# Moving the second block's context norm, keys and values from a layer's MLP to its attention

## The chip, the cores and the metric

One core of a Trainium2 chip runs the whole program as one launch. The metric is device microseconds of one execution, taken as the median over runs; lower is better. The engines of the core are TensorE (PE in the profile, its weight loads shown apart as PEld), VectorE (DVE), ScalarE (ACT), GpSimd (POOL) and SyncE (SP), whose queue issues nearly all DMA transfers. Each engine works through its own instructions in the order in which the program lists them for it.

## The reference, cut to what matters

Two transformer blocks run one after the other on 512 tokens of width 1024. The first has two layers: in each, three kinds of attention (sliding window, full grouped-query, and latent attention called MLA) over 512 latent and 256 context tokens, and a squared-ReLU MLP. The second block starts with differential attention beside a long convolution. Its attention also sees 256 context tokens of its own, `ctx_2`. What the change touches is only this: the norm of that context, and the keys and values made from it.

```python
a_ctx = _modulate(_rmsnorm(h_ctx, norm1_g[i]), mod_c[0], mod_c[1])          # 256 x 1024
kv_ctx = a_ctx @ mix_w_in[e][:, KV_START:HY_START] + mix_b_in[e][KV_START:HY_START]
k_c, v_c = _split_kv(kv_ctx)                                                # 256 x 512 each
k_all = jnp.concatenate([k_c, k_l], axis=1)
v_all = jnp.concatenate([v_c, v_l], axis=1)
```

`ctx_2` and the modulation depend on nothing that the first block computes, so this work may stand anywhere before the second block's attention.

## The kernel before, in words

Activations lie transposed, with 128 channels on the partitions and tokens along the free side; a 1024-wide vector is eight such tiles. Large products are made from a high and a low part of each operand (`mm3`, L645: hi·hi, hi·lo, lo·hi). Their weights are streamed in tiles of 128x1024: SP issues the load of `wraw` (L72), ACT casts the high part `whi` (L90), DVE subtracts for the low part `wlo` (L91). The context keys and values are the exception: they are plain fp32 matmuls with unsplit weights. One such matmul instruction on 256 columns shows as two records in the trace.

The program is written as generators that are stepped in turn, and a scheduler then fixes each engine's instruction list by the order of writing and priorities. Tiles come from pools with fixed numbers of slots, and a tile whose slot is still in use by an earlier one waits for the last user of that one: the large pool `B` has 21 slots, `Tm` (scratch of one 128x512 tile) four, `wm` (tiles of modulation weights) two. In PSUM, during the first block's attention, there are two double banks and four single ones (`P1`).

**Attention of the second layer** (about 1200 to 1400 us) is a list of 64 units, each a head and a stretch of queries. `attend` walks it with a lag: scores `s` (L257, mask L259) on PE, maximum and sums `st` on DVE, exponential `p` (L280) on ACT, normalisation `p` (L289) on POOL, transposes `pt` (L303) on PE, a high and a low copy `pth` (L330, ACT) and `ptl` (L335, DVE), the product `acc` with the values (L346), and its evacuation through a `Tm` tile `yt` (L349, ACT), an ACT copy `y` (L351) and a POOL addition (L352). Between units it calls `fill(i)`, which steps preparations: `prepare(p)` forms queries and keys of the MLA heads (`cn`, `cx`, `ck`, scratch tiles `w` and `u` in `Tm`, DMAs into `qc` and `kc`). Units 0 to 15 are full attention, 16 to 31 the window, 32 to 63 MLA.

**The MLP of that layer** (about 1505 to 1845 us) is stepped by `run(mlp, 0.8, 1.3)`: per step of the MLP it makes 0.8 steps of the modulation jobs and 1.3 steps of `self.jobs`, which `queue2` has filled with the filter of the long convolution and then `context_job`. That job loads `ctx_2` into two `B` tiles, sums squares (`RmsNorm.feed`: `rq` L203, `ns` L211, then sums over the channels on PE, `rv` L208 and L209), forms the inverse root (L632 to L637), applies norm and modulation (L1492 DVE, L1493 POOL), and makes the keys of four heads: eight matmuls each (L1502), bias into `ckx` (L1505, ACT), high and low parts stacked in `ckk` (L1553 ACT, L1554 DVE), a DMA to DRAM (`kctx`). Weights come by `SideStream` (tiles `wside`, each load paced by a small POOL copy).

**The transition** from that MLP to the second block (about 1863 to 1901 us) is a layer norm followed by the second block's own RMS norm. The loop over `self.side` steps it, and in between steps `context_values`: 32 matmul instructions (L1532, two double PSUM tiles), bias `cvx` (L1537, DVE), split `cvv` (L651 ACT, L652 DVE), DMA to `vctx`. Then the second block's projections `pj` begin.

## Time and profile before

| | before |
|---|---|
| median of three runs | 2979.42 us (2972.44 to 2990.2) |
| profiled execution | 2984.58 us, its span 2982.6 us |
| mean granted TensorE clock | 0.979 |
| PE busy | 2822.2 us, 95% of the span |
| DVE busy | 1973.3 us, 66% |
| ACT busy | 1235.4 us, 41% |
| POOL busy | 640.3 us, 21% |

The rows further down are read against the profiled execution. Busy time counts an engine's instructions, not its waits; a granted clock of 1.00 is TensorE's upper level (2.4 GHz), 0.50 its lower one (1.2 GHz). In a view of the chain, each step of the program's critical path is one line with its start and length; a step on PE that follows another on PE without a gap means that PE itself was the limit there.

### The profile page before, as it was taken

To read this page: it belongs to the slowest core of one execution; us is meant where nothing else is said; L and a number is where in the kernel's file an instruction comes from. 1 tells how busy PE (TensorE), PEld (TensorE's weight loads), DVE (VectorE), ACT (ScalarE), POOL (GpSimd) and SP (SyncE) were. 2 spreads that over 40 slices of the span, in tenths; PEclk is the share of its full clock that TensorE was granted. 3 is DMA by queue.
4 is the path that set the end of the run, shared out by engine and by line. 5 is a ranking of instruction groups with operands and counts; after the bars stand their busy time and mean duration, and the time that the engine had idled before them with its cause. 6 is when DMAs were issued, how large, how long until landed. Compare 5 with 4: busy or idle time off the path is not lost.

```text
span 2982.6 us, 40376 instructions
## 1 busy us (share of the span) xinstructions
PE 2822.2 (95%) x15212; PEld 2373.5 (80%) x15212; DVE 1973.3 (66%) x3193; ACT 1235.4 (41%) x2249; POOL 640.3 (21%) x780
## 2 busy tenths in 40 slices
PE   8988999999999989898999999998899999999998
PEld 5877778888888877777887788777688888888887
DVE  3677777775657476887687565768976754664445
ACT  3477663322222244776332332533653223543322
POOL 1034346300000061343601121312310000200001
PEclk8999999999999999999999999999999999999999
DMA  6022222344434221012145455233115542222222
GB/s 252 32 68 71 90 89 85 107 145 157 143 113 142 78 71 47 13 37 70 64 170 182 166 205 187 97 125 117 64 64 193 202 139 99 76 78 94 97 99 71
DMA packets 102218, 327.95 MB, mean 110 GB/s; under 512 B 11617, under 2 KB 18721, under 8 KB 102024
## 3 DMA queue, kind: packets, MB, share of 16 engines
q1 hardware_dynamic: 101448, 323.67, 31.3%
q8 instruction: 120, 1.97, 0.3%
q10 hardware_dynamic: 576, 1.71, 0.2%
q14 instruction: 74, 0.61, 0.1%
HBM read 306.98 MB, written 12.59 MB: 107 GB/s over the span
## 4 chain that ended last, share of the span: by engine, by line
PE 75%; DVE 11%; ACT 5%; issue 4%; DMA 2%; POOL 2%; DVEq 0%; ACTq 0%; POOLq 0%; SPq 0%
PE f L645 48%; PE pj L645 7%; PE op L645 5%; PE s L257 3%; PE acc L346 2%; PE pt L303 1%; DVE ptl L335 1%; DVE st L270 1%; DVE h L1088 1%; ACT p L280 1%; DVE wlo L91 1%; ACT pth L330 1%; PE ms L1112 1%; PE lv L180 1%; DVE R L174 1%
## 5 line engine op out<-in xcount | busy, mean ns | idle before, releaser
L90 ACT CAST whi<-wraw 128x1024 fp32r<-128x1024 f32 x342 | 357.6, 1046 | 1211.0 <-PE f L645 1000.7
L645 PE MATMUL f<-hn,whi 128*128 128x512 f32 (+1 forms) x2688 | 718.1, 365 | 8.3 <-ACT hn L1089 6.8
L91 DVE TENSOR_TENSOR wlo<-wraw,whi 128x1024 fp32r<-128x1024 f32 x342 | 422.8, 1237 | 325.7 <-ACT whi L90 319.1
L645 PE MATMUL f<-act,whi 128*128 128x512 f32 x2240 | 612.2, 371 | 1.6 <-DVE R L990 1.6
L645 PEld LDWEIGHTS f<-hn,whi 128*128 128x128 f32 x2688 | 467.0, 190 | 93.0 <-ACT hn L1089 8.0
L645 PEld LDWEIGHTS f<-act,whi 128*128 128x128 f32 x2240 | 388.9, 188 | 77.1 <-DVE R L990 2.8
L645 PE MATMUL f<-hn,wlo 128*128 128x512 f32 (+1 forms) x1344 | 447.3, 362 | 0.0
L645 PE MATMUL f<-act,wlo 128*128 128x512 f32 x1120 | 377.6, 370 | 0.0
L990 DVE SCALAR_TENSOR_TENSOR R<-f,modsb,R 128x512 f32<-128x512 f32 (+1 forms) x280 | 188.9, 693 | 161.2 <-PE f L645 160.9
L645 PEld LDWEIGHTS f<-hn,wlo 128*128 128x128 f32 x1344 | 239.2, 190 | 40.2
L574 DVE SCALAR_TENSOR_TENSOR wm<-wm,sbc 128x1024 f32<-128x1024 f32 x152 | 188.9, 1246 | 119.6 <-DMA wm<-wada_in 75.5
L645 PE MATMUL pj<-h,whi 128*128 128x512 f32 (+1 forms) x912 | 248.0, 372 | 11.1 <-ACT h L651 5.4
L564 POOL COPY wm<-act 128x1 f32<-128x1 f32 x144 | 78.7, 554 | 792.0 <-DVE wm L574 388.1
L645 PEld LDWEIGHTS f<-act,wlo 128*128 128x128 f32 x1120 | 195.4, 188 | 37.1
L645 PEld LDWEIGHTS pj<-h,whi 128*128 128x128 f32 x912 | 158.5, 193 | 47.3 <-issue 7.4
L289 POOL TENSOR_SCALAR p<-p,st 128x768 f32<-128x768 f32 (+2 forms) x160 | 130.3, 817 | 226.8 <-DVE st L287 180.8
L270 DVE TENSOR_REDUCE st<-s 128x1 f32<-128x768 f32 (+3 forms) x176 | 156.3, 889 | 31.2 <-PE s L257 19.3
L335 DVE TENSOR_TENSOR ptl<-pt,pth 128x256 fp32r<-128x256 f32 (+3 forms) x304 | 153.3, 535 | 18.8 <-ACT pth L330 15.4
L211 POOL TENSOR_TENSOR ns<-ns,rq 128x256 f32<-128x256 f32 x54 | 46.3, 867 | 479.8 <-ACT rq L203 478.7
L303 PE MATMUL pt<-ident,p 128*128 128x128 f32 x816 | 124.6, 281 | 23.1 <-DVE ptl L335 9.7
L645 PE MATMUL pj<-h,wlo 128*128 128x512 f32 (+1 forms) x456 | 145.5, 359 | 0.0
L280 ACT ACTIVATE p<-s,st 128x768 f32<-128x768 f32 (+2 forms) x160 | 125.8, 788 | 44.6 <-DVE st L270 34.3
(377 smaller groups left out, 4629.4 us busy)
## 6 DMA issues: line engine op xcount, KB each, us to landing
wraw<-fc_in SPq DMA_DIRECT2D x128, 512.0 KB, 3.4
wraw<-mlp_in SPq DMA_DIRECT2D x128, 512.0 KB, 3.2
wm<-wada_in SPq DMA_DIRECT2D x96, 512.0 KB, 4.0
wm<-wmod_in SPq DMA_DIRECT2D x56, 512.0 KB, 4.0
wraw<-win_in SPq DMA_DIRECT2D x24, 512.0 KB, 3.2
wm<-wmodk_in SPq DMA_DIRECT2D x24, 512.0 KB, 4.4
wn<-wmodk_in SPq DMA_DIRECT2D x16, 512.0 KB, 8.6
wraw<-wout_in SPq DMA_DIRECT2D x16, 512.0 KB, 3.2
```

What stands on the lines that cost most here:

```text
L90: nc.scalar.copy(out=hi[:, 0:n], in_=t[:, 0:n])
L91: nc.vector.tensor_tensor(out=lo[:, 0:n], in0=t[:, 0:n], in1=hi[:, 0:n].bitcast(F32), op=ALU.subtract)
L257: nc.tensor.matmul(self.s[:, a:b], lhsT=q, rhs=kk[:, k0:k0 + b - a], start=i == 0, stop=end)
L270: nc.vector.tensor_reduce(out=self.st[:, 0:self.nq], in_=s, axis=AX.X, op=ALU.max, negate=True)
L280: nc.scalar.activation(out=self.p[:, b * m:b * m + m], in_=self.s[:, self.c0 + b * m:self.c0 + b * m + m], func=AF.Exp, bias=st[:, b:b + 1 ...
L289: nc.gpsimd.tensor_scalar(out=self.p[:, b * m:b * m + m], in0=self.p[:, b * m:b * m + m], scalar1=st[:, 6 + b:7 + b], scalar2=1.0, op0=ALU ...
L303: nc.tensor.transpose(self.pt[t // w][:, t % w * 128:t % w * 128 + 128], self.p[:, t * 128:t * 128 + 128], k.ident)
L335: self.k.nc.vector.tensor_tensor(out=pr.lo[:, s0:s0 + c, q0:q0 + nq], in0=src, in1=pr.hi[:, s0:s0 + c, q0:q0 + nq].bitcast(F32), op=ALU.su ...
L564: self.nc.gpsimd.tensor_copy(out=t[:, 0:1], in_=self.gate)
L574: nc.vector.scalar_tensor_tensor(out=junk, in0=t, scalar=1.0, in1=s, op0=ALU.mult, op1=ALU.mult, accum_out=dst)
L645: self.nc.tensor.matmul(ps[:, c0:c1], lhsT=w, rhs=x[:, c0:c1], start=first and n == 0, stop=last and n == 2)
L990: nc.vector.scalar_tensor_tensor(out=zz, in0=ps[:, c0:c1], scalar=g(m0 + mi), in1=zz, op0=ALU.mult, op1=ALU.add)
```

## The change: what it does

The job for the context no longer stands in `queue2`. It is started ahead of the second layer's attention and stepped once by each `fill(i)` from unit 8 on; it has 34 steps, so it covers units 8 to 41 of 64. What is left at the end of the attention is drained there.

- `ctx_2` is loaded at the start of the job into the two `wm` tiles (one 512 KB DMA each), and stays there.
- One `B` slot, `cw`, holds the norm's scratch, then the weights (128x1024, one 512 KB load per key head, four for the values) and the value bias. So a load waits for the matmuls that read the load before it.
- Eight key matmuls per head stand together (L1515 of the changed kernel), eight value matmuls per load (L1528). The values of two heads are summed in one single PSUM bank over two loads, where there were double ones.
- `ckk` and `cvv` are now `Tm` tiles, where they were `B` tiles; each is held until its DMA has read it. There are four DMAs to `vctx` where there were two.
- The loop over `self.side` only steps the norms; the rate of `self.jobs` in the MLP goes from 1.3 to 0.9, for the filter alone.

The matmuls, their shapes and the number of evacuations are the same; 16 weight loads of 256 KB for keys and values become eight of 512 KB.

```diff
-RATES = [(1.3, 0), (0.8, 1.3), (1.1, 0), (1, 0)]
+RATES = [(1.3, 0), (0.8, 0.9), (1.1, 0), (1, 0)]
+CTX0 = 8
...
 class RmsNorm:
 
 
-    def __init__(self, k, z, c0, c1, first=FIRST):
+    def __init__(self, k, z, c0, c1, first=FIRST, s=None):
         self.k, self.z, self.c0, self.c1, self.n, self.first = k, z, c0, c1, c1 - c0, first
-        self.s = k.norm_space(self.n)
+        self.s = k.norm_space(self.n) if s is None else s
         self.ps = None
 
...
+        context = None
+        if last:
+            self.need("b0.m1")
+            context = self.context_job()
 
         def fill(i):
             next(rest, None)
+            if last and i >= CTX0:
+                next(context, None)
...
         self.attend(units, fill, LAG1, HOLD1, ATT1, ORD1)
+        if last:
+            self.drain(context)
...
             self.run(self.mlp(W, hn, z, gs, groups, sides, norm, finish, f"l{l}.g2"), *RATES[l])
-            if last:
-                self.need("ctxk")
-            for i, _ in enumerate(self.side):
-                if last and i >= VSKIP and (i - VSKIP) % VEACH == 0:
-                    for _ in range(VSTEP):
-                        next(self.values, None)
-            if last:
-                for _ in self.values:
-                    pass
+            for _ in self.side:
+                pass
...
 
         self.jobs.append(self.filter_job())
         bg.append(J(a["wada0"], range(16, 24), [(4, 0)], "b0.g1", "bada0"))
-        self.jobs.append(self.context_job())
...
     def context_job(self):
 
         nc, a = self.nc, self.a
-        t0, t1 = self.B([6, 256], F32, "c2"), self.B([2, 256], F32, "c2")
-        nc.sync.dma_start(out=t0, in_=a["ctx2"][:, 0:6, :])
-        nc.sync.dma_start(out=t1, in_=a["ctx2"][:, 6:8, :])
-        x = [t0[:, i, :] for i in range(6)] + [t1[:, i, :] for i in range(2)]
-        norm = RmsNorm(self, lambda m: x[m], 0, 256)
+        x = []
+        for i in range(2):
+            t = self.wm.tile([128, 1024], F32, name="wm", tag="wm").rearrange("p (k t) -> p k t", k=4)
+            nc.sync.dma_start(out=t, in_=a["ctx2"][:, 4 * i:4 * i + 4, :])
+            x += [t[:, k, :] for k in range(4)]
+        slot = self.B([1536], F32, "cw")
+        w, vb = slot[:, 0:1024], slot[:, 1024:1536]
+        norm = RmsNorm(self, lambda m: x[m], 0, 256, s=slot[:, 0:768].rearrange("p (a b) -> p a b", a=3))
+        for _ in range(2):
+            yield
         for m in range(8):
             norm.feed(m)
-        yield
+            if m % 2:
+                yield
         self.fold(14, 5, 0, 1, "n1g0", None)
 
         def apply(m, t, r):
             nc.vector.tensor_tensor(out=t, in0=t, in1=r, op=ALU.mult)
             nc.gpsimd.tensor_scalar(out=t, in0=t, scalar1=self.dcol(14, m), scalar2=self.dcol(15, m), op0=ALU.mult, op1=ALU.add)
 
-        yield from norm.finish(apply)
-        W = SideStream(self, [a["mixk"][hd][:, h * 512:h * 512 + 512] for hd in range(4) for h in range(2)])
+        for i, _ in enumerate(norm.finish(apply)):
+            if i % 2 == 0:
+                yield
+        nc.sync.dma_start(out=vb, in_=a["vbias"])
+
+        def load(src):
+            nc.sync.dma_start(out=w, in_=src)
+            for _ in range(2):
+                yield
+
         for hd in range(4):
+            yield from load(a["mixk"][hd])
             ps = self.P1("ck")
-            for h in range(2):
-                w = W.get()
-                for k in range(4):
-                    nc.tensor.matmul(ps[:, 0:256], lhsT=w[:, k * 128:k * 128 + 128], rhs=x[4 * h + k], start=h + k == 0, stop=h == 1 and k == 3)
-                yield
-            X = self.Tm("ckx")
+            for k in range(8):
+                nc.tensor.matmul(ps[:, 0:256], lhsT=w[:, k * 128:k * 128 + 128], rhs=x[k], start=k == 0, stop=k == 7)
+            X, kt = self.Tm("ckx"), self.Tm("ckk", F32R)[:, 0:512].rearrange("p (a b) -> p a b", a=2)
             nc.scalar.activation(out=X[:, 0:256], in_=ps[:, 0:256], func=AF.Identity, bias=self.col("mixbk", hd), scale=1.0)
-            kt = self.B([2, 256], F32R, "ckk")
             self.stack_key(X[:, 0:256], [kt[:, 0, :], kt[:, 1, :]])
             self.dma(a["kctx"][:, hd, :, :], kt)
             yield
-        self.values = self.context_values(x)
-        for _ in range(VPRE):
-            next(self.values)
-            yield
-        self.done.add("ctxk")
-        yield
-
-    def context_values(self, x):
-        nc, a = self.nc, self.a
-        W = SideStream(self, [a["mixv"][i][:, h * 512:h * 512 + 512] for i in range(4) for h in range(2)])
-        vb = self.B([512], F32, "vb")
-        nc.sync.dma_start(out=vb, in_=a["vbias"])
-        for _ in range(VPRE):
-            W.load()
-            yield
         for g in range(2):
-            ps = self.P2("cv")
-            for i in range(4):
-                w = W.get()
-                for kk in range(2):
-                    k = 2 * i + kk
+            ps = self.P1("cv")
+            for i in range(2):
+                yield from load(a["mixv"][2 * g + i])
+                for kk in range(4):
+                    k = 4 * i + kk
                     for t in range(2):
-                        nc.tensor.matmul(ps[:, 512 * t:512 * t + 256], lhsT=x[k][:, t * 128:t * 128 + 128], rhs=w[:, kk * 256:kk * 256 + 256],
-                                         start=k == 0, stop=k == 7)
-                yield
+                        nc.tensor.matmul(ps[:, t * 256:t * 256 + 256], lhsT=x[k][:, t * 128:t * 128 + 128], rhs=w[:, kk * 256:kk * 256 + 256],
+                                         start=k == 0 and t == 0, stop=k == 7 and t == 1)
             xs = self.Tm("cvx")
             for t in range(2):
-                nc.vector.tensor_tensor(out=xs[:, t * 256:t * 256 + 256], in0=ps[:, 512 * t:512 * t + 256], in1=vb[:, g * 256:g * 256 + 256], op=ALU.add)
-            v = self.B([2, 2, 256], F32R, "cvv")
+                nc.vector.tensor_tensor(out=xs[:, t * 256:t * 256 + 256], in0=ps[:, t * 256:t * 256 + 256], in1=vb[:, g * 256:g * 256 + 256], op=ALU.add)
             xv = xs[:, 0:512].rearrange("p (t h d) -> p h t d", t=2, h=2)
             for h in range(2):
-                hi, lo = (v[:, h, q, :].rearrange("p (t d) -> p t d", t=2) for q in range(2))
+                v = self.Tm("cvv", F32R)[:, 0:512].rearrange("p (q n) -> p q n", q=2)
+                hi, lo = (v[:, q, :].rearrange("p (t d) -> p t d", t=2) for q in range(2))
                 self.split(hi, lo, xv[:, h])
-            self.dma(a["vctx"][:, 2 * g:2 * g + 2, :, :], v)
+                self.dma(a["vctx"][:, 2 * g + h, :, :], v)
             yield
         self.done.add("ctx2")
         yield
```

On PE in the window part of the attention, where queries of MLA heads are prepared (`cn`, `cx`; `kk` and `q` are keys and queries of the window, `va` its values), there stands before:

```order
L645 MATMUL cn<-cq,whi 128x512 x2
L645 MATMUL cn<-cq,wlo 128x512
L303 MATMUL pt<-ident,p 128x128
L257 MATMUL s<-kk,q_10375 128x256 x4
L259 LDWEIGHTS maskt
L259 MATMUL s<-maskt 128x128
L303 MATMUL pt<-ident,p 128x128 x9
L346 MATMUL acc<-pth,va 128x256 x3
L645 MATMUL cx<-cq,whi 128x512 x2
```

and now:

```order
L645 MATMUL cn<-cq,whi 128x512 x2
L645 MATMUL cn<-cq,wlo 128x512
L303 MATMUL pt<-ident,p 128x128 x5
L257 MATMUL s<-kk,q_10375 128x256 x4
L259 LDWEIGHTS maskt
L259 MATMUL s<-maskt 128x128
L1515 MATMUL ck<-wm,cw 128x256 x8
L645 MATMUL cx<-cq,whi 128x512 x2
L645 MATMUL cx<-cq,wlo 128x512
```

The second head's eight key matmuls now stand in front of `cx`, and the transposes and the product that stood there have moved. The first head's batch stands some thirty rows earlier, the third some thirty later, the fourth at the start of the MLA units and the four value batches among these.

On PE at the end of the transition, from the last sums of the norms to the second block's projections, there stands before (`c` is the normalised context):

```order
L209 MATMUL rv<-rq,ones 128x256
L1532 MATMUL cv<-wside,c_15888 128x256 x2
L209 MATMUL rv<-rq,ones 128x256
L1532 MATMUL cv<-wside,c_15888 128x256
L209 MATMUL rv<-rq,ones 128x256
L1532 MATMUL cv<-wside,c_15888 128x256 x6
L1532 MATMUL cv<-wside,c_15889 128x256 x4
L645 MATMUL pj<-h,whi 128x512 x3
```

and now:

```order
L180 MATMUL lv<-lq,ones 128x256 x2
L209 MATMUL rv<-rq,ones 128x256
L180 MATMUL lv<-lq,ones 128x256 x2
L209 MATMUL rv<-rq,ones 128x256 x13
L645 MATMUL pj<-h,whi 128x512 x2
L645 MATMUL pj<-h,wlo 128x512
```

All value matmuls are gone from there, and only sums of the norms are left on PE ahead of `pj`.

On SP in the attention, the transfers of the values' weights (`mixv`) and of the split values now stand between those of the MLA heads (`qc`, from `w` and `u`); before, the `qc` rows there followed one another:

```order
L1507 DMA cw<-mixv_in 128x1024 x2
L658 DMA vctx<-cvv 128x512 x2
L1507 DMA cw<-mixv_in 128x1024
L658 DMA qc<-w 32x512
L658 DMA qc<-u 32x512
```

The last load of `mixv` stands ahead of four `qc` transfers; it waits until the third batch of value matmuls has read the slot.

## Rows read from the trace of the kernel before

**Rows 1.** The page: busy time of each engine over the whole span.

```profile
PE 2822.2 (95%) x15212; PEld 2373.5 (80%) x15212; DVE 1973.3 (66%) x3193; ACT 1235.4 (41%) x2249; POOL 640.3 (21%) x780
```

**Rows 2.** Busy time by stretch: attention units 8 to 41, MLP, transition.

```profile
core 0: us, PE busy (x) PEld busy (x) DVE busy (x) ACT busy (x) POOL busy (x), PEclk, DMA share, GB/s
1219.00:1322.00 103.00, 92.53 (x604) 81.02 (x604) 84.12 (x217) 78.34 (x210) 43.82 (x53) 0.93 0.10 27
1505.00:1845.00 340.00, 337.66 (x1434) 268.45 (x1433) 230.97 (x331) 104.94 (x148) 56.73 (x77) 1.00 0.53 183
1874.00:1901.00 27.00, 25.91 (x113) 20.29 (x111) 20.08 (x51) 19.67 (x52) 8.61 (x10) 1.00 0.32 117
```

**Rows 3.** Chain of waits, late MLP and transition: start, us, step, records.

```profile
1777.60 1.73 PE ck L1502 x8
1779.33 5.45 PE f L645 x24
...
1896.91 4.32 PE cv L1532 x20
```

**Rows 4.** Tiles of keys and values: count, ns min/median/max, first and last start.

```profile
L1502 PE MATMUL ck<-c,wside x64: 376/379/380, 1777.4 to 1834.6; 128*128 128x256 f32 x64
L1532 PE MATMUL cv<-wside,c x64: 378/379/380, 1874.0 to 1900.8; 128*128 128x256 f32 x64
L1505 ACT ACTIVATE ckx<-ck,colsb x4: 457/470/475, 1786.5 to 1835.1; 128x256 f32<-128x256 f32 x4
L1553 ACT CAST ckk<-ckx x8: 395/403/408, 1787.1 to 1836.0; 64x256 fp32r<-64x256 f32 x8
DMA to landing us min/median/max: 3.2/3.2/3.2
```

**Rows 5.** Lines of the context norm in the MLP: busy us, mean ns.

```profile
L1493 POOL TENSOR_SCALAR c<-c,der 128x256 f32<-128x256 f32 x8 | 6.6, 832 | 7.8 <-DVE c L1492 7.8
L211 POOL TENSOR_TENSOR ns<-ns,rq 128x256 f32<-128x256 f32 x6 | 6.2, 1027 | 9.1 <-ACT rq L203 8.7
L1492 DVE TENSOR_TENSOR c<-c,ns 128x256 f32<-128x256 f32 x8 | 3.3, 461 | 0.0
L203 ACT ACTIVATE rq<-c 128x256 f32<-128x256 f32 x7 | 2.7, 415 | 3.2 <-POOL ns L211 3.2
```

**Rows 6.** Timeline, end of the transition: start, us, engine, operation, [wait].

```profile
1896.74 4.48 PE L1532 MATMUL cv<-wside,c 128*128 128x256 f32 x20
...
1900.10 1.28 DVE L1088 SCALAR_TENSOR_TENSOR h<-R,der,ns 128x256 f32<-128x256 f32 x3
1900.62 1.31 ACT L1089 ACTIVATE h<-h,der 128x256 fp32r<-128x256 f32 x3 [1.62 <-DVE h L1088]
...
1901.18 1.14 PE L645 MATMUL pj<-h,whi 128*128 128x512 f32 x3
```

**Rows 7.** Busy time by stretch inside the attention (columns as in Rows 2).

```profile
1222.00:1239.00 17.00, 15.96 (x114) 14.72 (x113) 13.86 (x28) 14.01 (x33) 7.89 (x10) 0.94 0.06 17
1260.00:1270.00 10.00, 7.80 (x54) 6.50 (x53) 7.18 (x21) 6.04 (x20) 4.11 (x5) 1.00 0.10 21
1270.00:1280.00 10.00, 7.43 (x43) 6.16 (x43) 8.58 (x25) 6.89 (x18) 2.85 (x4) 0.76 0.21 47
1290.00:1300.00 10.00, 9.98 (x68) 8.89 (x67) 8.05 (x19) 8.13 (x21) 5.94 (x8) 1.00 0.01 2
1310.00:1320.00 10.00, 7.29 (x38) 6.03 (x37) 8.05 (x12) 4.82 (x10) 3.30 (x3) 0.83 0.46 134
```

**Rows 8.** Timeline: where the first preparation's `cx` ran.

```profile
1263.60 0.73 PE L645 MATMUL cx<-cq,whi 128*128 128x512 f32 x2
```

**Rows 9.** Two stretches in which PE waits, then fills (columns as in Rows 2).

```profile
1210.00:1220.00 10.00, 6.05 (x22) 4.51 (x22) 9.79 (x15) 6.80 (x13) 2.36 (x2) 0.52 0.00 0
1220.00:1230.00 10.00, 9.62 (x60) 8.96 (x59) 7.91 (x18) 6.89 (x16) 4.34 (x5) 0.80 0.10 27
```

**Rows 10.** Waits in 1205 to 1410: total us, times, longest.

```profile
ACT yt L349 <- PE acc L346: 11.7, 11, 3.2
```

More of the change, by code (lines that the diff above doesn't have):

```diff
@@ L51 @@
 HN = ((1, 2), (1, 1))
-VPRE, VSTEP, VSKIP, VEACH = 3, 1, 16, 2
 PRI_W, PRI_EVAC, PRI_MOD = 0, 300, -500
```

## The prediction, made before the changed kernel ran

> **What bounds the kernel now.** I read the engines' shares first: PE is busy 95% of the span [rows 1], so work that leaves PE helps only where PE was the limit, and work given to PE is free only where it waited. So next the stretches between which work moves [rows 2]. In the MLP, PE is busy 337.66 of 340 us at granted clock 1.00, and its chain goes from an MLP piece to a key piece without a gap [rows 3]: PE alone sets the time. In attention units 8 to 41 PE is busy 92.53 of 103 us, at clock 0.93: idle 10.5 us, in which softmax steps on the other engines come late. The reader should see that this is where the work goes, and that "idle tiles" offers PE 10.5 us there and no more. The idle is uneven [rows 7]: 2.2 and 2.6 us in the two tens from 1260 to 1280, 2.7 us in 1310 to 1320, almost nothing at 1290 to 1300. In the transition PE is busy 25.91 of 27 us [rows 2], but that needs the timeline: there the values fill waits that other engines set.
>
> **What leaves the MLP.** The keys are 64 records [rows 4], shown on the chain in pieces of 8 in 1.73 us [rows 3], 0.216 us each (a record's 0.379 us overlaps its neighbours): 64 × 0.216 = 13.8 us. Four channel sums of the norm are of the same 128x256 form: 0.9 us. Nothing hides these; the gain is **14.7 us**. The keys' ACT, DVE and POOL work leaves too, worth nothing since PE has no gap. The filter job stays: 58 MLP steps × 0.9 make 52 job steps (counted in the code), it needs 50, so none is left to run after the MLP. SP's list loses 16 loads of 256 KB from a stretch with DMA busy 0.53 [rows 2]: nothing.
>
> **What leaves the transition.** 64 records of values, again 64 × 0.216 = 13.8 us of PE time. But the last 20 run from 1896.74 for 4.48 us, while ACT writes the last `h` from 1900.62 after waiting for DVE, and `pj` starts at 1901.18 [rows 6]. The `h` chain of DVE and ACT, not the values, ends last. Without the values `pj` starts about as before. What may be gained is DVE and ACT time in front of `h`: four `cvx` (bounded by a 128x256 subtraction, 0.461 us [rows 5]) and their splits, partly after `pj` already: 0.2 to 3 us. Against it stands the clock. Without the values PE is busy only about 12 of 27 us. In 1210 to 1220, where PE was busy 6 of 10 us, the granted clock was 0.52, the lower level, and in the next 10 us, with PE nearly full, 0.80 [rows 9]; so `pj` could begin slow and lose up to 3 us. The nearest other rows, 1260 to 1270 (busy 7.8, clock 1.00) and 1270 to 1280 (7.4, 0.76) [rows 7], show it not to be sure. I take a **net cost of 1.5 us**, between −1.5 (a gain) and +3.
>
> In a sentence beside the sum: the Trainium skill ("TensorE: Matmul & The Clock Gate", section "What's actually happening") tells of a default throttled state that activity releases. Rows 9 agree, 0.52 and then 0.80; by that page alone the end at 3 us would be the one to take, 1.5 us more than I do.
>
> **What comes into the attention.** The same 64 + 64 records and four sums, 132 × 0.216 = 28.5 us of PE time. If all 10.5 us of idle took it up, 18.0 us would be added; if none, 28.5. The order decides between them, since each batch stands at one place of PE's list: eight batches of 16 records, 3.46 us each.
> - The first and the fourth key batch and the first two of values stand in full stretches (the latter near 1290 to 1300, PE 9.98 of 10 [rows 7]): 4 × 3.46 = 13.8 us, and 0.9 us for the sums.
> - The second key batch stands just ahead of the first preparation's `cx`, at 1263.60 [rows 8], the third some 10 us behind. These stretches idle 4.8 us [rows 7], for transposes and scores that wait for softmax. A batch also delays what feeds the next softmax, so I count 3 of their 6.9 us as hidden: 3.9 us.
> - The last two value batches stand by the second preparation, where 1310 to 1320 idles 2.7 us: again 3 of 6.9 hidden, 3.9 us.
>
> That is 22.5 us, in the middle of 18.0 and 28.5. Filled gaps may raise the granted clock from 0.93: I take 1 us back, and up to 4, as the whole deficit is 0.07 × 103 = 7 us and much of it lies in waits.
>
> The other engines. ACT gets eight squares (0.415 each [rows 5]), four `ckx` (0.470), eight casts (0.403 [rows 4]) and about six more of 0.4: 3.3 + 1.9 + 3.2 + 2.4 = 10.8 us. DVE gets eight multiplications of 0.461 [rows 5] and some 18 operations of that size or less: under 12 us. POOL gets 6.6 + 6.2 = 12.8 us [rows 5]. Idle in the stretch are 24.7 us on ACT, 18.9 on DVE, 59 on POOL [rows 2], and it becomes over 20 us longer: on average covered. Not so at its head, where the norm's squares, roots and applications stand: in 1222 to 1239 ACT is busy 14.01 of 17 us, DVE 13.86 [rows 7]. The norm's 4.6 us of ACT exceed the 3 us that are left by 1.6: add 1.5 us. Sum: 22.5 − 1 + 1.5 = **23.0 us** (16 to 29).
>
> The queues. SP is moved past eight loads of 512 KB, each of which waits until the batch before has read the slot, and behind the last `mixv` load stand the `qc` transfers that scores wait for. A transfer of `ckk` took 3.2 us from issue to landing [rows 4]; the price is 0 to 4 us. I take 0, as the last value batch stands ahead of these scores on PE itself and would wait for the same load. The two early loads of the context stand in SP's list at the end of the first layer's MLP, behind the modulation loads that free their slots, with `wraw` loads behind them. They add 1 MB, 5.7 us at the 183 GB/s that the MLP shows [rows 2]; the stream is loaded ahead there, so I take 0, and 5.7 us at most. Moving the PE pieces out of the second MLP lets that weight stream run 4% tighter, with DMA at 0.53 [rows 2]: nothing.
>
> **Sum.** +23.0 in the attention, +1.5 in the transition, −14.7 in the MLP: +9.8, some 10 us. Against the profiled 2984.6 us (span 2982.6 and 2.0 around it) that is 2994.4. The profiled run lies 5.2 us over the median of 2979.4, so I put the forecast on the median: **2989 us**. A measurement of this kernel can tell about 0.5%, 14.9 us, from no change.
>
> **Rivals.**
> - *Gaps and clock swallow more.* All 10.5 us of idle are used and the clock gives back 2 to 4: the attention costs 14 to 18, net −2 to +3, 2977 to 2982 us. For it: the batches stand near the gaps. Against: four of eight stand in full stretches.
> - *No gap takes any.* In the attention PEld is busy 81.02 of 103 us, 79%; in the saturated MLP 268.45 of 340, also 79% [rows 2]. If weight loads are the measure, the attention is as full as the MLP: cost 28.5, net 28.5 + 1.5 − 14.7 = +15.3, 2995 us. Beside it: the Trainium skill ("Perfetto Trace Analysis", section "Identifying the Most-Contended Engine") says to judge TensorE by its LDWEIGHTS row. Against it: at 1290 to 1300, with PE full, PEld was busy 8.89 of 10 [rows 7], so 79% is no ceiling in the attention, whose matmuls are shorter.
> - *Scratch becomes the limit: slower.* `ckx`, `ckk`, `cvx` and `cvv` come into `Tm`, four slots shared with `w`, `u` and `yt`. A `ckk` or `cvv` keeps its slot until its DMA has landed, 3.2 us [rows 4]. If a preparation's `w` and `u` hold two more, `yt` (which frees the PSUM bank of `acc`) has to wait on ACT, and the `pth` copies of the next units queue behind it, for which PE waits. Now `yt` waits for `acc` itself alone, 11.7 us in 11 cases [rows 10]. Priced at 1 to 2 us for each of the four `ckk` and two `cvv` pairs, 6 to 12 us more: +16 to +22, about 2998 us. It decides once PE waits for `pth` behind a `yt` in over three places. Against: a unit takes 3 us (103 us for 34), so a slot is back within about one.
> - *The values did set the transition's end.* The chain of waits does end in `cv`, 4.32 us [rows 3]. If `h` came late only because `cvx` and `cvv` held DVE and ACT, 8 us go: net about 0, 2980 us. Against: rows 6.
> - *It doesn't do what it says:* the order shows that it does.
>
> **How the numbers follow.** The forecast 0.55; gaps swallow more 0.15; no gap 0.11; scratch 0.13; values 0.04; something else 0.02. The low end is 2975 (the second case, with the lower bound of the transition), the high end 3003 (scratch at its dearest); outside I leave 0.18. Faster by over 0.5% needs 2964.5, where the attention would have to take nearly all for nothing: 0.04. Slower by over 0.5% begins at 2994.3: nearly all of scratch, half of "no gap" and a seventh of the forecast's own spread, 0.26. The rest, 0.70, is within 0.5%.
>
> **What would show it.** The MLP shorter by 14 to 15 us with no `ck` pieces on the chain; `pj` starting as soon after the last `op` as before, within 3 us; the stretch from unit 8 to 41 some 23 us longer, with PE idle about 6 of some 126 us, less than its 10.5. Longer waits of ACT `yt` for DMA, or of PE for `pth`, would speak for scratch. The prediction is wrong if PE's idle time in the attention grows, or if the transition shortens by over 5 us.

## The result, and the profile after

The changed kernel takes 3000.4 us in the median of eight runs, the kernel before 2978.5 us in as many: a ratio of 1.0074, interval 1.0060 to 1.0088, 22 us (18 to 26) slower. The forecast was 2989 us, some 10 us slower. 3000.4 lies in its range (2975 to 3003), and in the part over 0.5% slower, to which it gave 0.26.

The page of the changed kernel, its engines' busy time ([rows 1] is the same line of before):

```profile
PE 2818.3 (94%) x15212; PEld 2366.9 (79%) x15212; DVE 1977.9 (66%) x3193; ACT 1236.4 (41%) x2249; POOL 633.0 (21%) x774
```

PE does as many instructions in 4 us less of busy time, and the program is longer: more of it is waits. To find it, I cut the program at places that both traces have, by PE's timeline: the first product `acc` of the attention, the first `op` after the last unit, the first `op<-act` at the end of the MLP, the last of those, the first `pj` of the second block, and the first `ut` behind it. "Attention" is then from 1221.83 to 1407.90 us before and from 1212.46 to 1429.00 after. The view of busy time by stretch (columns as in [rows 2]) gives for these, first the kernel before:

```profile
1221.83:1407.90 186.07, 166.01 (x1100) 146.28 (x1098) 149.52 (x333) 143.05 (x357) 78.05 (x91) 0.95 0.15 42
```

and the changed kernel, with two pieces in which the context's norm stands:

```profile
1212.46:1429.00 216.54, 193.94 (x1232) 168.59 (x1230) 162.40 (x360) 154.15 (x384) 86.59 (x105) 0.97 0.21 67
1226.00:1240.00 14.00, 10.37 (x77) 8.85 (x77) 10.01 (x25) 9.75 (x26) 8.46 (x13) 1.00 0.00 1
1240.00:1252.00 12.00, 9.21 (x67) 8.10 (x68) 12.00 (x38) 8.71 (x29) 6.61 (x11) 1.00 0.12 46
```

The attention is 30.5 us longer: 27.9 us more PE busy time, for the 132 records that came, and 2.5 us more idle (20.1 to 22.6). On the whole no idle time was filled. Part of the 30.5 us belongs to the mark: from the first scores `s` to the first `acc` the changed kernel takes 44.4 us and the kernel before 45.9, and the traces do not tell why. Counted from the first projection `pj` of that layer to the first `op`, the two take 325.9 and 354.9 us, 29.0 more:

```profile
1081.96:1407.90 325.94, 288.83 (x1778) 247.29 (x1776) 255.40 (x490) 218.69 (x490) 119.22 (x134) 0.95 0.16 48
1074.10:1429.00 354.90, 313.31 (x1910) 266.52 (x1908) 268.26 (x517) 229.69 (x517) 127.75 (x148) 0.98 0.20 63
```

In the two pieces with the norm PE is idle 3.6 of 14 and 2.8 of 12 us. The timelines of PE, POOL and ACT there (start, us, engine, operation, in brackets what ended the wait) show the first of them:

```profile
1228.88 0.70 PE L208 MATMUL rv<-cw,ones 128*128 128x256 f32 x2 [2.77 <-POOL cw L211]
1229.42 0.59 PE L209 MATMUL rv<-rq,ones 128*128 128x256 f32 x2
1229.85 1.62 PE L303 MATMUL pt<-ident,p 128*128 128x128 f32 x12
```

```profile
1226.32 0.90 POOL L289 TENSOR_SCALAR p<-p,st 128x768 f32<-128x768 f32 x1
1227.31 0.72 POOL L352 TENSOR_TENSOR y<-y,yt 64x256 f32<-64x256 f32 x1
1228.11 0.72 POOL L211 TENSOR_TENSOR cw<-cw,rq 128x256 f32<-128x256 f32 x1
```

```profile
1230.05 0.47 ACT L632 ACTIVATE cw<-rv,eps 128x256 f32<-128x256 f32 x1 [2.19 <-PE rv L209]
1230.56 0.42 ACT L634 ACTIVATE cw<-cw 128x256 f32<-128x256 f32 x1
1230.88 0.84 ACT L330 CAST pth<-pt 128x512 fp32r<-128x512 f32 x2
```

The last of the norm's seven additions (L211) stands on POOL behind the softmax's `p` and `y`. PE stands at the sum that needs it, with the units' transposes `pt`, which do not need it, behind the sum. ACT stands at the root that needs the sum, and the copies `pth` of these transposes stand behind the root. In the second piece DVE is busy 12.00 of 12 us: there L1498 applies the norm among the softmax's own DVE steps. In the view of the chain (start, us, step), every step from 1237.65 to 1248.94 is on DVE, and 2.5 us of them are L1498:

```profile
1237.81 0.56 DVE wm L1498
...
1238.44 0.72 DVE st L270
1239.17 0.60 DVE ptl L335
...
1240.21 0.79 DVE wm L1498 x2
...
1243.09 1.15 DVE wm L1498 x2
```

In the kernel before DVE was nearly as full at this place, some 70 us behind the first scores, but PE hardly waited, and its chain runs mostly over PE and ACT there (columns as in [rows 2]):

```profile
1244.00:1254.00 10.00, 9.65 (x76) 8.48 (x74) 9.17 (x34) 8.47 (x28) 4.40 (x7) 1.00 0.01 3
```

The other parts of the program: from the first `op` to the first `op<-act` (layer norm and MLP) 437.8 us before, 424.2 after, 13.7 less; from the last `op` to `pj` 29.9 and 30.9, 1.0 more; from `pj` to `ut` 43.9 and 45.7, 1.8 more. The sum is 29.0 − 13.7 + 2.8 = +18.1 us, at the low end of the interval of the times (19.6 us with the attention cut at `acc`).

### The profile page after: what moved, and what is told of

It reads as the page before. It is cut to its first block, busy times and chain, and to the rows that moved or that the text cites. A ratio compares the mean times of both kernels' runs of the same rounds, so it can differ in the third digit from the quotient of the medians.

```text
span 2992.5 us, 40313 instructions
## 1 busy us (share of the span) xinstructions
PE 2818.3 (94%) x15212; PEld 2366.9 (79%) x15212; DVE 1977.9 (66%) x3193; ACT 1236.4 (41%) x2249; POOL 633.0 (21%) x774
## 4 chain that ended last, share of the span: by engine, by line
PE 74%; DVE 12%; ACT 6%; issue 3%; POOL 2%; DMA 2%; DVEq 0%; SPq 0%; POOLq 0%; ACTq 0%
PE f L645 47%; PE pj L645 7%; PE op L645 6%; PE s L257 2%; PE acc L346 2%; PE pt L303 1%; DVE h L1088 1%; DVE st L270 1%; ACT p L280 1%; DVE ptl L335 1%; DVE wlo L91 1%; ACT pth L330 1%; DMA wm<-wada_in 1%; PE ms L1112 1%; DVE R L174 1%
## 5 line engine op out<-in xcount | busy, mean ns | idle before, releaser
L270 DVE TENSOR_REDUCE st<-s 128x1 f32<-128x768 f32 (+3 forms) x176 | 156.0, 888 | 29.7 <-PE s L257 22.0
L211 POOL TENSOR_TENSOR ns<-ns,rq 128x256 f32<-128x256 f32 x48 | 40.8, 860 | 512.4 <-ACT rq L203 486.8
```

The lines of the kernel that those rows point to most:

```text
L270: nc.vector.tensor_reduce(out=self.st[:, 0:self.nq], in_=s, axis=AX.X, op=ALU.max, negate=True)
```

## The experiments

One table for all; "ratio" is to runs of the kernel before on the same chip, "attention" and the other lengths are cut as above, "idle" is attention less PE's busy time in it, and "from layer's `pj`" is the length from the layer's first projection to the first `op`. The attention's length repeats to 0.2 us between the three kernels with no context work in it (186.1, 186.1, 186.0), and to 1.2 us between the three with the changed kernel's attention (216.5, 216.6, 217.7). That is much better than whole runs: the same code ahead of it ended anywhere between 1168 and 1177 us. So sizes are read from it, none under some 1 us, and the times only decide the whole. Each kernel has one trace. e2, e7, e10, e12 and e13 also set the rate of the jobs in the MLP to 1.0, where the changed kernel has 0.9; what the rate does is tried in e9.

| kernel | ratio (95%) | from layer's `pj` | attention | idle | to `op<-act` | `op` to `pj` | `pj` to `ut` |
|---|---|---|---|---|---|---|---|
| before | 1 | 325.9 | 186.1 | 20.1 | 437.8 | 29.9 | 43.9 |
| changed | 1.0074 (1.0060-1.0088) | 354.9 | 216.5 | 22.6 | 424.2 | 30.9 | 45.7 |
| e1, no context work | 0.9986 (0.9969-1.0002) | 326.1 | 186.1 | 19.9 | 428.5 | 31.0 | 45.6 |
| e2, values back | 0.9997 (0.9983-1.0010) | 343.6 | 203.8 | 24.4 | 419.1 | 29.9 | 43.9 |
| e3, no norm | 1.0059 (1.0037-1.0082) | 348.4 | 210.0 | 16.3 | 424.9 | 30.5 | 46.9 |
| e8, norm early | 1.0050 (1.0032-1.0067) | 348.7 | 208.5 | 16.3 | 424.8 | 30.5 | 45.6 |
| e5, sums on PE | 1.0096 (1.0081-1.0112) | 356.1 | 216.3 | 18.5 | 428.3 | 31.1 | 45.7 |
| e6, filler | 1.0056 (1.0042-1.0070) | 356.1 | 217.7 | 22.4 | 424.9 | 29.7 | 44.1 |
| e9, rate 1.3 | 1.0074 (1.0056-1.0091) | 355.0 | 216.6 | 22.7 | 420.3 | 31.1 | 45.6 |
| e10, values back, norm early | 0.9996 (0.9983-1.0009) | 337.2 | 197.0 | 18.2 | 420.8 | 29.9 | 43.9 |
| e7, keys in the layer norm | 0.9999 (0.9986-1.0012) | 326.2 | 186.0 | 20.2 | 433.8 | 29.9 | 43.9 |
| e11, small pieces | 1.0026 (1.0015-1.0036) | 341.8 | 201.7 | 13.7 | 426.6 | 31.1 | 45.7 |
| e12, small pieces, values back | 0.9999 (0.9988-1.0011) | 339.0 | 198.9 | 20.9 | 419.2 | 29.9 | 43.9 |
| e13, keys in the transition | 1.0006 (0.9992-1.0021) | 335.8 | 195.7 | 16.9 | 420.8 | 33.4 | 44.1 |

**e1: the context work left out.**

```diff
-            context = self.context_job()
+            context = self.no_context()   # writes zeros to kctx and vctx
```

> The changed kernel without the context work: keys and values of the second block's context are written as zeros, so no norm, no matmuls and no weight loads for them. What is left is the attention, MLP and transition of the changed kernel with nothing moved in. Theory A (the work costs more in the attention than the forecast's 23 us: the trace shows 31 us from the first unit to the last): about 31 us less than the changed kernel, 2969 us, some 9 to 10 us below the kernel before (ratio 0.997). Theory B (the attention cost the forecast's 23 us and the rest of the loss lies elsewhere, in the MLP or behind the transition): 2977 us, no different from before (ratio 0.9995).

Measured: 0.9986; the attention is as long as before to 0.1 us. So the whole 30.5 us there is the context work and its waits, as theory A has it. In time the work costs 0.88% of 2980, 26 us, between the theories; e1 keeps the longer transition (31.0 and 45.6), and its MLP stretch is 4 us longer than the changed kernel's: the wait for `R` of which e9 tells is 3.1 us there and 2.1 in the changed kernel, and there is another of 1.2 us.

**e2: the values back in the transition.**

```diff
-RATES = [(1.3, 0), (0.8, 0.9), (1.1, 0), (1, 0)]
+RATES = [(1.3, 0), (0.8, 1.0), (1.1, 0), (1, 0)]
...
+        self.jobs.append(self.values_job())     # loads the normalised context from DRAM
...
-            for _ in self.side:
-                pass
+            for i, _ in enumerate(self.side):
+                if last and i >= VSKIP and (i - VSKIP) % VEACH == 0:
+                    for _ in range(VSTEP):
+                        next(self.values, None)
```

> Half of the change: norm and keys in the attention, the values back among the norms of the transition, as before (the normalised context goes through DRAM in between). Theory A (the value batches cost nearly their whole PE time in the attention, and the transition lost its filler and with it PE's clock): 11 to 14 us less in the attention and 2 to 3 less in the transition, 2984 to 2987 us, ratio 1.002 to 1.003. Theory B (the values were mostly hidden in the attention, and keys and norm are what costs): 3 to 6 us less, 2995 us or more, ratio 1.0055.

Measured: 0.9997, no slower than before. The attention gives back 12.8 us (11.3 counted from the layer's `pj`), the transition and the projections behind it 2.8, exactly what they had lost, and the MLP 5.0 more. Those 5.0 are not the values': the rate of the jobs is 1.0 here, and the wait of which e9 tells is gone. Theory A, with more than it asked for. In time the whole loss is undone. By the trace some 14 of 19 us of that come from the values, which had been moved out of a place where they cost nothing, and the rest goes with the rate.

**e3: the norm left out; e8: the norm beside the projections.**

```diff
-            norm.feed(m)
...
-        for i, _ in enumerate(norm.finish(apply)):
+        for i in range(9):
```

In e8 each projection steps the job, for its first eleven steps:

```diff
-CTX0 = 8
+CTX0 = 19
+CTXN = 11
...
+            self.hook = [context, CTXN]
```

> The changed kernel with the context's norm left out: keys and values are formed from the raw context, at the same units. Theory A (the norm costs 5 to 7 us there, because ACT waits at the root for the channel sum with the copies of the units queued behind it): 2993 to 2995 us, ratio 1.005, and the units before the first key batch come as early as in the kernel before. Theory B (the norm costs only its four sums, 0.9 us, and the batches all the rest): 2999 to 3000 us, ratio 1.007.

> The changed kernel with the norm stepped by the projections ahead of the attention, where ACT, DVE and POOL have room and PE has none; the key and value batches stand at the same units as in the changed kernel. Theory A (the norm costs by a wait in the attention, not by its own work): 4 to 6 us less than the changed kernel, 2994 to 2996 us, ratio 1.0055. Theory B (its work costs the same anywhere, or it costs next to nothing): within 1 us of the changed kernel, ratio 1.007.

Measured: attention 210.0 and 208.5, 6.6 and 8.0 us less. In both PE's idle falls from 22.6 to 16.3:

```profile
1213.06:1423.02 209.96, 193.68 (x1229) 169.18 (x1227) 156.24 (x349) 150.38 (x373) 77.79 (x91) 0.96 0.22 69
```

```profile
1211.13:1419.68 208.55, 192.29 (x1229) 168.24 (x1227) 156.21 (x349) 150.36 (x373) 77.76 (x91) 0.97 0.21 65
```

The first row is e3, the second e8. PE's busy time changes by 0.3 and 1.7 us, its idle time by 6.3: the norm costs by waits, theory A. Not all of e8's 8.0 us is a gain, since there the norm stands ahead of the mark: e8 takes 97.4 us from the layer's first `pj` to the first scores, where the changed kernel takes 94.0, and wins back 1.7 of these 3.5 us before the first `acc`.

The first scores of the changed kernel, whose `pj` starts at 1074.10, and of e8, whose `pj` starts at 1071.00:

```profile
1168.09 0.96 PE L257 MATMUL s<-kk,q 128*128 128x512 f32 x4 [0.89 <-ACT raw L676]
```

```profile
1168.44 1.28 PE L258 MATMUL s<-kk,q 128*128 128x512 f32 x4
```

And e8 from that `pj` to `op`, to be read against the 354.90 us of the changed kernel:

```profile
1071.00:1419.68 348.68, 314.13 (x1911) 268.11 (x1909) 267.25 (x517) 230.12 (x517) 129.26 (x148) 0.97 0.20 64
```

From the layer's `pj` on, e3 is 6.5 us shorter than the changed kernel and e8 6.2: that is what the norm costs among the units. The time says so for e8, narrowly (1.0050, 7 us off the changed kernel, with intervals that just overlap); e3's interval holds both theories. Without the norm 3.8 us of the 20.1 us of idle are used by the batches, so they do fill gaps, a little.

**e5: the norm's squares summed on PE.**

```diff
-        norm = RmsNorm(self, lambda m: x[m], 0, 256, s=...)
+        norm = RmsNorm(self, lambda m: x[m], 0, 256, first=0, s=...)
```

> The changed kernel with the context norm's squares summed on PE (16 records of 128x256 instead of four) and not by seven additions on POOL. Theory A (of the norm's 6 to 8 us in the attention the larger part is the root on ACT, which waits for a sum that stands behind POOL's softmax work): 12 more records cost 2.6 us on PE, the wait of PE and ACT for POOL (2.8 and 2.2 us) goes, the attention is about as long as in the changed kernel or 1 to 3 us shorter: 213 to 216 us. Theory B (the norm costs by DVE and ACT work of its own, which delays softmax): the attention 2 to 3 us longer, 219 us. Either way within 3 us of the changed kernel in all, ratio 1.0065 to 1.0085; the attention's length decides.

Measured: the attention 216.3 us, as long as the changed kernel's within what such lengths tell, with 3.8 us more PE work and 4.1 us less idle. PE's wait for POOL (2.8 us) and ACT's wait at the root (2.2) are gone. So that chain over POOL, PE and ACT could be removed, as theory A has it, but paying it off with PE work gains nothing. How much of the 4.1 us was the chain's, and how much was idle time that the new work filled, this run does not tell apart. The whole program was slower by more than the attention says (four runs, with an interval that overlaps the changed kernel's); in its profile 4.1 us of that are in the MLP, which this kernel does not alter, and where the wait for `R` of which e9 tells is 3.1 us instead of 2.1.

**e6: a filler without use in the transition.**

```diff
+                        self.nc.tensor.matmul(ps[:, 512 * t:512 * t + 256], lhsT=self.ident, rhs=w, start=k == 0, stop=k == 7)
```

> The changed kernel with 32 matmul instructions without a use (128x256, from constants that lie in SBUF, results never read) in the transition, at the steps at which the values' matmuls stood before. Theory A (the transition got longer by 2.8 us because PE, without the values, falls to a lower granted clock there and the sums and first projections run slowly): the transition and the first projections as long as in the kernel before, the granted clock 1.00 where the changed kernel has 0.84, 2.8 us less in all, 2997 to 2998 us, ratio 1.0065. Theory B (the loss comes from something else, or the filler takes the place of what it gains): within 1 us of the changed kernel or above it, ratio 1.0075 or more. The difference is near what the times can tell; the granted clocks and the stretches of the trace decide.

Measured: 29.7 and 44.1 us where the changed kernel has 30.9 and 45.7, and the kernel before 29.9 and 43.9. The same 27 us of the transition, first of the changed kernel, then with the filler (columns as in [rows 2], whose last row is the kernel before):

```profile
1881.43:1908.43 27.00, 15.31 (x49) 10.84 (x48) 18.02 (x44) 19.25 (x49) 8.60 (x10) 0.83 0.27 97
```

```profile
1887.33:1914.33 27.00, 25.91 (x114) 20.38 (x112) 19.26 (x47) 19.70 (x51) 8.60 (x10) 1.00 0.27 98
```

ACT and DVE do nearly the same; PE's work and its granted clock differ. The stretch behind it, from `pj` to `ut`, shows what the clock alone is worth, 1.6 us, since PE is busy in all of it and has the same work, first in the changed kernel, then with the filler:

```profile
1909.60:1955.25 45.65, 45.65 (x193) 36.87 (x194) 26.91 (x41) 15.75 (x24) 12.84 (x18) 0.96 0.23 81
1914.29:1958.36 44.07, 44.07 (x194) 35.90 (x194) 26.93 (x41) 15.75 (x24) 13.12 (x18) 1.00 0.24 84
```

Useless work on PE shortens transition and projections by 2.8 us, theory A: the value matmuls had been free there and more than free. In time 5 us are gained, with intervals that overlap.

**e9: the rate of the jobs as before.**

```diff
-RATES = [(1.3, 0), (0.8, 0.9), (1.1, 0), (1, 0)]
+RATES = [(1.3, 0), (0.8, 1.3), (1.1, 0), (1, 0)]
```

> The changed kernel with one number undone: the rate of the jobs in the second MLP 1.3 again, where the change made it 0.9, so the filter's steps stand earlier in the MLP. Theory A (at 0.9 a burst of the filter's DVE work falls on the first evacuations of the MLP's second product, PE waits 2.1 us for DVE there and its clock falls behind it): no such wait, 3 to 5 us less, 2996 us, ratio 1.006. Theory B (that wait moves with the burst, or was a matter of the one execution): the MLP as long as in the changed kernel, within 1 us, ratio 1.0074.

In the changed kernel PE waits once early in the MLP. Its timeline, and DVE's ahead of it:

```profile
1547.22 0.73 PE L645 MATMUL f<-act,whi 128*128 128x512 f32 x2 [2.13 <-DVE R L990]
```

```profile
1540.24 2.11 DVE L1577 SCALAR_TENSOR_TENSOR fhd<-fhd,sn 64x512 f32<-64x512 f32 x3
1542.28 1.21 DVE L91 TENSOR_TENSOR wlo<-wraw,whi 128x1024 fp32r<-128x1024 f32 x1
1543.41 0.68 DVE L1577 SCALAR_TENSOR_TENSOR fhd<-fhd,sn 64x512 f32<-64x512 f32 x1
...
1546.42 0.74 DVE L990 SCALAR_TENSOR_TENSOR R<-f,modsb,R 128x512 f32<-128x512 f32 x1
```

`fhd` is the filter job; at the lower rate its burst falls between the evacuations `R` of the MLP's second product, for whose PSUM PE waits. The 40 us around it, changed kernel and then e9:

```profile
1529.00:1569.00 40.00, 37.87 (x160) 30.80 (x160) 35.42 (x55) 10.28 (x13) 3.96 (x6) 0.96 0.50 173
```

```profile
1538.28:1578.28 40.00, 40.00 (x175) 32.20 (x173) 33.61 (x50) 12.59 (x16) 2.98 (x6) 1.00 0.62 204
```

Measured: the wait is gone and the stretch to `op<-act` is 3.9 us shorter, as theory A says. The time of the whole did not move (1.0074); 4 us are at the edge of what its interval tells, so only the traces bear this out. They all do: the seven kernels with the rate 0.9 have this wait, 2.1 to 3.1 us at the same place, and take 424.2 to 428.5 us to `op<-act`; the five with 1.0 or 1.3 and no keys in that stretch do not have it and take 419.1 to 420.8.

**e10, e7: less and less left in the attention.**

e10 is e2 and e8 together. e7 adds that the keys are stepped by the layer norm's generators ahead of the MLP, with weights loaded during the attention's output projection:

```diff
+            sides = [self.along(s, self.keys) for s in sides]
```

> Of the change only the keys in the attention: the norm beside the projections ahead of it, the values back in the transition. Theory A (norm 8 us and values 13 us of the attention's extra 30, transition 3): the attention some 10 us longer than in the kernel before, the MLP some 15 to 18 us shorter, 2972 to 2976 us, ratio 0.998. Theory B (parts do not add up, since each takes the same waits): 2981 us or more, no better than with the values back alone, ratio 1.000.

> Nothing left in the attention: the norm beside the projections ahead of it, the keys' matmuls among the layer norm between the attention and the MLP, where PE waits some 6 us and shows a granted clock of 0.83 in 20 us, the values back in the transition. Theory A (there the keys take the place of waits of PE, as the values do in the transition, and in the attention they did not, since it has other work in its list): attention as before, the layer norm 4 to 8 us longer, the MLP 14 to 18 us shorter: 2968 to 2974 us, ratio 0.996 to 0.997. Theory B (the keys delay the norm's sums on PE, and their evacuation its ACT and DVE, so they cost their 13.8 us there too): 2979 to 2981 us, ratio 1.000.

Measured: both as fast as the kernel before (0.9996, 0.9999), theory B in time. In e10 the keys alone cost the attention 11.0 us. In e7 the attention is untouched, but the stretch to `op<-act` is 13.0 us longer than in e10: the keys cost nearly what they cost in the MLP, 13.8. PE has gaps in that layer norm too, and they stay: in the 50 us around it PE is idle 5.7 us in the kernel before and 5.2 us in e7.

```profile
1452.90:1502.90 50.00, 44.26 (x243) 38.11 (x243) 42.46 (x63) 24.62 (x46) 34.02 (x36) 0.93 0.23 76
1447.42:1497.42 50.00, 44.84 (x255) 39.79 (x254) 37.55 (x62) 25.29 (x52) 31.52 (x36) 0.93 0.17 58
```

That the norm's sums are held up because they stand in PE's list behind the keys is argued from that list and was not tried.

By its stretches e10 is what theory A says: the attention 11.0 us longer, the MLP 17.1 shorter. And counted from the layer's `pj` the parts add up, which theory B denied: e7, with only the norm beside the projections, is 0.2 us longer than the kernel before; the keys add 11.0 (e10 less e7), the values 11.5 (e8 less e10; 11.3 by e2), and the norm among the units 6.2 (the changed kernel less e8). The sum is the 29.0 us.

**e11, e12: batches cut into pieces of two instructions.** e11 is e8 with keys and values cut, e12 is e10 with the keys cut.

```diff
+                if k in (1, 3, 5):
+                    yield
```

> The norm beside the projections as in e8_early_norm, and the key and value batches cut into pieces of two matmul instructions, one piece for each unit from the 12th on, where they stood eight together. Theory A (eight together, 3.5 us, are longer than any wait of PE, so most of a batch delays what PE waits for; pieces of 0.9 us fit): the attention 3 to 6 us shorter than with the norm alone moved (208.5), 203 to 205 us, and PE's idle time in it down from 16 to 11 us. Theory B (PE's waits end a chain through ACT and DVE that starts from PE itself, so any piece put into PE's list lengthens the chain): 207 to 209 us. In all 2990 to 2997 us, ratio 1.003 to 1.005.

> As e10_values_norm (norm beside the projections, values back in the transition), the keys in the attention in pieces of two. Theory A (small pieces fit into PE's waits): the attention 3 to 5 us shorter than there (197), 192 to 194 us, in all 4 us less than before to 8 less, ratio 0.9975 to 0.999. Theory B (they do not): 196 to 197 us, ratio 0.9996 as there.

Measured: e11 has the attention at 201.7, 6.9 less than e8, idle 13.7, clock 0.99:

```profile
1226.75:1428.44 201.69, 187.95 (x1229) 163.98 (x1227) 158.60 (x349) 151.43 (x373) 78.10 (x91) 0.99 0.22 67
```

Its ratio is 0.24% under that of e8, with intervals that just overlap: theory A. But e12, with the keys alone in pieces, has 198.9, where eight together had 197.0: theory B. So small pieces paid only where values were among them. In e11 these also ran later, in units 35 to 58 where they had run to unit 41, and in both kernels the keys start seven units earlier than in e8 and e10; size of the piece and place were not tried apart.

**e13: the best that these pointed to.**

In e10, values and keys change places: the values in pieces of two from unit 35 on, the keys' eight half heads where the values stood.

```diff
+CTX0 = 35
...
+                    if kk < 3:
+                        yield
```

> The best that the runs so far point to: the norm beside the projections, the values in the attention but in pieces of two instructions and late (one piece for each unit from the 35th on), the keys' matmuls in the transition in the place that the values had before (two double PSUM tiles, as there). Theory A (the values' pieces fit late in the attention, as the difference of 2.8 us between the attentions of e11_fine and e12_fine_keys says, and PE work of any kind is free in the transition): attention 189 to 192 us where the kernel before has 186, MLP as in e10_values_norm, transition as before (29.9 and 43.9 us): 8 to 12 us less than before, ratio 0.996 to 0.997. Theory B1 (the values cost late what they cost at units 30 to 41): attention 197 to 199 us, ratio 0.9995. Theory B2 (the keys have more work for ACT and DVE after them, which holds up the norms there): the transition 2 to 5 us longer, ratio 0.998.

Measured: 1.0006, as fast as the kernel before. The attention is 195.7, 9.6 us for the values, between theories A and B1, so the 2.8 us that I had from e11 less e12 did not add up. The keys lengthen the transition by 3.5 us, as theory B2 has it: ACT is busy 25.5 us from the last `op` to `pj`, where it is 21.6 with the values there (e10), and `pj` waits 2.0 us for ACT's `h`. No kernel tried here beats the one before beyond its interval. By the stretches of their traces, from the layer's `pj` to `ut`, e7, e10 and e12 are 4 to 6 us shorter than it, which their times do not bear out; whether that lies outside these marks or in the one trace of the kernel before stays open.

## Why the prediction was right or wrong

The direction and the range were right, and so was most of the mechanism: PE work moved from a full stretch to one that is nearly full, against a place in the transition where it was free. The size was about half of what came, and one part of the mechanism failed by the forecast's own sign: it named a rise of PE's idle time in the attention as what would make it wrong, had it fall to about 6 us in units 8 to 41, and over the whole attention it rose by 2.5 us. That 3000.4 lies in the range is in part luck, since the high end, 3003, was the price of a scratch limit that did not come, and that by its own terms sums to 3001. By its terms:

- **MLP, forecast −14.7, came −13.7**, from two misses that cancel. That nothing of the keys was hidden fits. But the filter job was put at "nothing": the new rate moves a burst of it onto the evacuations, 3.9 us (e9). Without that the stretch is 17 to 19 us shorter than before (e2, e9, e10, e12), more than 14.7. Before, too, had one wait for `R`, 1.6 us at 1585.5, where DVE's list stood at a modulation step that waited 2.2 us for its DMA; e9 has 0.5 us at that place and e2, e10 and e12 none. What removed it was not tried.
- **Transition, forecast +1.5, came +2.8** with the projections behind it. The row taken against the clock [rows 9] was the right one, and the end of 3 us the right end; the gain of `cvx` set off against it did not show, as the filler, without `cvx`, takes the same 73.8 us to `ut` as the kernel before. The `h` chain ends last, as [rows 6] say: the changed kernel's `pj` starts after a wait for it.

```profile
1909.60 0.79 PE L645 MATMUL pj<-h,whi 128*128 128x512 f32 x1 [4.04 <-ACT h L1089]
```

  The Trainium skill ("TensorE: Matmul & The Clock Gate", section "What's actually happening") has throttling as the default and activity as what lifts it; here the trace agrees, 0.83 without and 1.00 with work that had no other use.
- **Attention, forecast +23.0, came +29.0** counted from the layer's `pj` (30.5 from `acc`). The keys, 10.8 us by the forecast, measure 11.0 (e10 less e7), and the values, 10.8 too, 11.3 to 11.5 (e2; e8 less e10). So of each 13.8 us of PE time 2.3 to 2.8 were hidden, where 3 were expected: that account held. The 1 us that the clock was to give back on top is not seen. The term that was mis-sized is the norm: 0.9 us of PE and 1.5 of ACT, measured 6.2 to 6.5 (e8, e3). I had weighed its work against the busy time of ACT, and the excess of 1.6 us. What costs is its order: a sum over eight tiles that goes through POOL, PE and ACT, each with the units' own work before and behind it in its list, so that each engine stands still for the one ahead (2.8 us of PE at the sum; e5 removes that wait). The rest I put down to DVE, full while the norm is applied. The chain from 1237 to 1249 has DVE as what held up the units there, and it was not tried alone.
- **Rival "scratch becomes the limit".** Its number, 2998, is nearest to what came, its mechanism is not there: ACT's `yt` waits less than before [rows 10], and for `acc` alone. From 1175 to 1429 the view of waits lists no engine that waits for a DMA, and no wait of PE for `pth`:

```profile
ACT yt L349 <- PE acc L346: 6.9, 10, 1.6
```

  That part was not tried by a run; the trace alone decides it. The same view bears out the queue's price of 0 in the attention. The two early loads of the context, issued at 981 and 989 us, show no price either: from the first layer's first `op` to its first `op<-act` the changed kernel takes 602.0 us, the kernel before 609.4, and e1, without these loads, 602.7.
- **Rival "no gap takes any"** comes out nearly right in the sum (28.5 us), as PE's idle in the attention did not fall, and wrong in its reason: without the norm 3.8 us of gaps are taken (e3, e8), in small pieces 6.3 (e11). PEld is busy 168.59 of 216.54 us after, 78%, and 163.98 of 201.69, 81%, in e11, so 79% was no ceiling. The Trainium skill ("Perfetto Trace Analysis", section "Identifying the Most-Contended Engine") judges TensorE's headroom by MFU or by the busy share of LDWEIGHTS. The second, 79% in both, does not tell this attention's room from the MLP's; PE's idle time does, 10.5 of 103 us against 2.3 of 340 [rows 2].
- **Rival "gaps and clock swallow more"** did not come. Its sum was off as well: 14 to 18 us with +1.5 and −14.7 make +0.8 to +4.8, not −2 to +3.
- **"The values set the transition's end"**, rejected: taking them away made it longer.
- The forecast took 0.5%, 14.9 us, as what a measurement can tell from no change; with eight runs of each the interval was 4 us to either side.

## What to carry to other kernels

Before moving work out of a full stretch, look at what it does where it stands: the value matmuls, run while PE waited for a norm, cost nothing there and held up the clock for what follows. That does not make every norm a free place: the keys cost 3.5 us in the same transition, by the ACT and DVE work behind them (e13), and 13.0 in the layer norm ahead of the MLP (e7). A stretch's idle time is not room for a chain: a small reduction that passes over three engines in their lists stops each of them in turn, so bill the chain by its waits, and put it where those engines have few other customers. When a side job's rate is changed with it, bill where the remaining job's bursts now fall. And when work is moved ahead of a mark, measure from a mark that lies ahead of both places.

## What the runs showed that I had not expected

That matmuls without any use make the program's next stage start earlier: 64 records more on PE, and the transition with the projections behind it 2.8 us shorter (e6). And that the length of one stage repeats to 0.2 us, at worst 1.2 us, between kernels and chips, while the whole program's time varies by 10 to 20 us from run to run: effects of 2 us could be read from the stage that the runs made here do not show.
